# Key and value products from unsplit fp32 operands, and a reordered start, in a two-layer gated attention block

## The chip, the cores and the metric

The kernel runs on one core of a Trainium2 chip. The metric is the device time of one execution in microseconds, the median of several runs. The profile is of one further execution.

## The reference

Two layers over 528 tokens (16 learned ones in front of 512) of width 1024, all in fp32. The parts that matter here:

```python
def hybrid_layer(x, norm_g, w_in, qn_g, kn_g, ...):
    h = rms_norm(x, norm_g)
    proj = jnp.einsum('btd,de->bte', h, w_in)
    q, k, v, gate_a, u_b, gate_b, q_idx, k_idx, w_idx, merge = jnp.split(proj, ...)
    q = apply_rope(rms_norm(q, qn_g), cos, sin)       # 8 heads of 64
    k = apply_rope(rms_norm(k, kn_g), cos, sin)       # one head of 64
    q_idx, k_idx = apply_rope(q_idx, ...), apply_rope(k_idx, ...)
    attn = indexer_sparse_attention(q, k, v, q_idx, k_idx, w_idx, k_top)   # top 128 keys by index score
    y_a = einsum(attn * silu(gate_a), w_a)
    y_b = einsum(multiscale_pool(u_b, ...) * silu(gate_b), w_b)
    g_a, g_b = split(sigmoid(merge))
    return x + einsum(g_a * y_a + g_b * y_b, w_out)
```

The keys `k`, the values `v`, the index key `k_idx` and the index weights `w_idx` are 64 + 64 + 64 + 8 = 200 columns of the input projection.

## The kernel before, in words

**Layout.** The residual `RES` holds the activations transposed: 8 tiles of 128 model dimensions on the partitions, 528 tokens along the free dimension. Tokens are cut in five tiles `TOK` (16, then four of 128) and two halves (the first 272, the last 256).

**Split products.** Most products are made from fp32r operands: an operand is split into a high part (a cast on ScalarE) and a low part (a subtraction), and a product is three matmuls, high by high, low by high, high by low. The normed activations are `nf` (fp32), `hhi` and `hlo`. A weight chunk is fetched as two fp32 halves `raw` (four buffers, so two chunks at a time) and split into tiles `w` (eight buffers, four to a chunk).

**Weights.** `chunks` lists all weight chunks in order of use. `w_load` fetches the next one, on SP's queue. `w_prep_enqueue` puts the splitting of the next one into `prep_q`, whose items run one at each `group_done`; `chunk()` runs what is left and hands the tiles out. When a chunk has been split its `raw` buffers are free and the next `w_load` is issued.

**Order.** The order of instructions on TensorE and VectorE is that of the code. `later(fn, n)` delays a function by n groups. ScalarE, GpSimd and SP are put in order by the scheduler. A row of scales or a transposed tile goes through a PSUM bank (`bank`: three of "d", four of "a", one of "v").

**The start of layer 0.** SP fetches an identity, the 16 tokens, the gains, two x tiles, the key-value chunk, two more x tiles, the rope tables, the head gains and the first index chunk, in that order. `x_half(0)` (L961) squares and sums each x tile on ScalarE, transposes it on TensorE and copies it to `RES`. The key-value chunk is split by ScalarE and GpSimd (L177, L180). `norm_half(0, 0, ...)` (L448) makes `nf` on VectorE (a multiplication by the gain and a row of scales in PSUM), `hhi` on ScalarE, `hlo` on VectorE, two steps behind.

`tok_trio` (L480) then makes keys and values of token tiles 0 to 2 (the first half) side by side: 24 steps of three matmuls of 200 columns. In its middle it calls a hook, which in layer 0 is the work on the other x tiles: `x_half(1)` and the head tables `tables(0)` on GpSimd (L421). Behind it stand `kv_post` (rope, norm and splitting of the keys) and `norm_half(0, 1, ...)`, the norm of the other half. Then come groups of 24 matmuls with `tok_group` (L468): index queries of tiles 1 and 2, keys and values of tiles 3 and 4 (`wk`), index queries of tiles 3 and 4, and the second index chunk, whose splitting is enqueued after the key-value group of tile 4.

**Layer 1** has the same order. Its first norm half is made during layer 0's output projection, where the key-value chunk is split as well; its hooks are the sums of squares and the norm of the second half. Its head tables, `tables(1)`, are issued after layer 0's last gate (L1190), though two of its five instructions run much earlier, where the scheduler found room.

All instructions of TensorE and VectorE are recorded through a helper and have line L60 in the profile; they are told apart by their tiles.

Of the kernel before, what the change touches and what calls it, by code (L numbers as in the profile page):

```python
# [8 lines left out]
F32 = mybir.dt.float32  # L9
# [24 lines left out]
LAG0 = 2  # L34
# [53 lines left out]
def tile_block(ctx: ExitStack, tc: tile.TileContext, x, meta, w_in, pool_w, w_a, w_b, w_out, rows, hgain, c_tab, out):  # L88
# [22 lines left out]
    chunks = []  # L111
    mixed, by_dma = set(), set()
    for l in range(2):
        wi = w_rows(w_in[l], 0, w_in.shape[2])
        chunks.append([(wi[:, :, 512:640], 0), (wi[:, :, 2688:2816], 128)])
        mb = [3784, 4040, 4296, 4552]
        order = [2176, 2432, 1664, 1920, 1408, 1152, 0, 640, 896, 256]
        chunks += [[(wi[:, :, c:c + 256], 0)] for c in order]
        chunks += [[(w_rows(w_b[l], c, 512), 0)] for c in (0, 512)]
        by_dma |= set(range(len(chunks) - 10, len(chunks)))  # L120
        mixed |= set(range(len(chunks), len(chunks) + 8))
        chunks += [[(wi[:, :, c:c + 256], 0)] for c in (*mb, 2760, 3016, 3272, 3528)]
        chunks += [[(w_rows(w_a[l], c, 512), 0)] for c in (0, 512)]
        chunks += [[(w_rows(w_out[l], c, 256), 0)] for c in (0, 256, 512, 768)]
# [3 lines left out]

    def w_load():
        c = W["load"]  # L130
        if c >= len(chunks):
            return
        W["load"] += 1
        kt = chunks[c][0][0].shape[1]
        cols = 2048 // kt
        raws[c] = []
        for s in range(2):
            r = wpool.tile([128, kt // 2, cols], F32, tag="raw", name="raw", bufs=4)
            for src, o in chunks[c]:
                nc.sync.dma_start(r[:, :, o:o + src.shape[2]], src[:, s * kt // 2:(s + 1) * kt // 2, :])  # L140
            raws[c].append(r)

# [11 lines left out]

    def w_prep_enqueue(eng=dve, casts_first=False):
        c = W["prep"]
        if c >= len(chunks):
            return
        W["prep"] += 1
        kt = chunks[c][0][0].shape[1]  # L160
        cols = 2048 // kt
        ready[c] = {}
        if c in mixed:
            prep_q.extend(mixed_prep(c))
            return
        parts = ready[c] = ([], [])

        def split(which):
            t = w_tile().rearrange("p (k e) -> p k e", e=cols)
            parts[which].extend(t[:, k] for k in range(kt // 2))  # L170
            return t

        his = {}

        def high(s):
            his[s] = split(0)
            act.copy(his[s], raws[c][s])  # L177

        def low(s):
            eng.tensor_sub(split(1), raws[c][s], f(his[s]))  # L180
# [12 lines left out]

        def plus(s):
            t = split(0)
            act.copy(t, raws[c][s])
            if s == 1:
                del raws[c]
                w_load()

        def highs():
            high(0)
            high(1)

# [172 lines left out]
    dma(xt[:, 1, :], x[0, 128:256, :])  # L377
    w_load()
    for t in range(2, 4):
        dma(xt[:, t, :], x[0, t * 128:(t + 1) * 128, :])  # L380
    dma(consts[:, 128:], c_tab[:, 128:])
    dma(gains, bass.AP(tensor=hgain.tensor, offset=hgain.offset, ap=[[0, 128], [128, 2], [64, 2], [1, 64]]))
    w_load()
    ident = consts[:, 0:128]
# [35 lines left out]

    def tables(l):  # L421
        gk = tmp.tile([128, 64], F32, tag="gk", name="gk", bufs=1)
        gp.tensor_scalar(gk, gains[:, 1, l], -0.125, None, op0=OP.mult)
        gq = gains[:, 0, l]
# [8 lines left out]
        for tab, g, w in ((Ck, gk, Sk), (Cq, gq, Sq)):  # L433
            gp.tensor_tensor(tab, ctab, bc(g), op=OP.mult)
            gp.tensor_tensor(w.rearrange("p t (a d) -> p t a d", a=2), s4, sw(g), op=OP.mult)

# [30 lines left out]

    def tok_group(t, w, e=256):  # L468
        s, m = TOK[t]
# [9 lines left out]

    def tok_trio(w, mid):  # L480
        hi, lo = H
        pss = [bank("v"), bank("d"), bank("d")]
        first, last_ = range(KT // 2), range(KT // 2, KT)
        for a, b, ks in ((hi, w[0], first), (lo, w[0], first), (hi, w[0], last_), (lo, w[0], last_),
                         (hi, w[1], range(KT))):
            if a is hi and ks is last_:
                mid()
            for k in ks:
                for t in range(3):
                    s, m = TOK[t]  # L490
                    pe.matmul(pss[t][:m, :KV], a[:, k, s:s + m], b[k][:, :KV], start=a is hi and b is w[0] and k == 0,
                              stop=b is w[1] and k == KT - 1)
        return pss

    def dense(w, mt_, a, n, rhs=H, kt=KT, late=False):
# [382 lines left out]
    def mix_gates(zb, ta, s0, n2, operands, splits, alos):  # L878
        base = popped[0] - progress[W["use"]]
        end_ = [None]  # L880
        for q in range(8):
# [23 lines left out]
            def gate(eh, t, src, in_sheet):  # L905
                j = 2 * q + eh
                cs = slice(s0 + t * n2, s0 + (t + 1) * n2)
                if q < 4:
                    th = src if in_sheet else sheet(n2, "th")[:, :n2]
                    act.activation(th, src, AF.Tanh, scale=0.5)  # L910
                    d = zb[:, j, cs]
                    later(lambda: dve.scalar_tensor_tensor(d, th, 1.0, d, op0=OP.add, op1=OP.mult), 2)
                else:
                    end_[0] = act.activation(ta[j - KT][:, cs], src, AF.Tanh, scale=0.5).ins

# [37 lines left out]
            ready.pop(c)  # L953
        return end_[0]

# [5 lines left out]
    def x_half(hf, after=None):  # L961
# [9 lines left out]
        for t in ts_:  # L971
# [3 lines left out]
            for k0 in range(0, KT, kk):  # L975
                tp = bank("v" if t == 0 else "a")
                for k in range(kk):
                    c = (k0 + k) * 128
                    pe.transpose(tp[:, k * m:(k + 1) * m], src[:, c:c + 128], ident[:m, :m])
                (act.copy if (t, k0) == (2, 0) else dve.tensor_copy)(  # L980
                    RES[0][:, k0:k0 + kk, s:s + m], tp[:, :kk * m].rearrange("p (k c) -> p k c", k=kk))
# [5 lines left out]
    x_half(0)  # L987
    w_prep_enqueue(gp)
    flush_prep()
    halved = norm_half(0, 0, rstd, LAG0, ())  # L990

    def second_x():
        x_half(1, halved)
        tables(0)

    hooks = {0: second_x, 1: lambda: norm_half(0, 1, rstd, LAG1)}

    for l in range(2):
        full = [(0, 0, HB, 0), (1, HB, T - HB, 0)]
        halves = full if l == 0 else [(1, 16, T - 16, 0)]  # L1000

        wk = chunk()
        KI[0] = one.tile([128, 2, T], F32R, tag="C", name="KI")
# [7 lines left out]

        pss = tok_trio(wk, hooks[0])
        flush_prep()
        w = chunk(ahead=False)
        for t in range(3):
            later(lambda t=t, ps=pss[t]: kv_post(l, t, ps), 1)
        group_done()
        hooks[1]()
        for what, t in (("q", 1), ("q", 2), ("k", 3), ("k", 4), ("q", 3), ("q", 4)):
            if what == "k":  # L1020
                ps = tok_group(t, wk, KV)
                later(lambda t=t, ps=ps: kv_post(l, t, ps), 1)
            else:
                index_queries(t, 0, w)
            group_done()
            if (what, t) == ("k", 4):
                w_prep_enqueue(casts_first=True)
        w = chunk()
# [154 lines left out]

        gates_end = mix_gates(zb, ta, s0, n2, operands, splits, alos)
# [150 lines left out]
```

## Time and profile before

| | |
|---|---|
| median of 3 runs | 772.63 us (771.91 to 772.87) |
| the profiled execution | 774.25 us |
| its span (first to last instruction) | 772.5 us |
| mean granted TensorE clock | 0.991 |
| TensorE matmul busy | 754.8 us (98%), 5989 instructions |
| VectorE, ScalarE, GpSimd busy | 557.9 (72%), 475.0 (61%), 235.4 (30%) us |
| HBM | 66.41 MB read, 8.55 MB written |

All times in views of the trace are microseconds from the start of the span. In the chain a row is start, length, engine, tile written and line; in the timeline it is start, busy time, engine, line, operation, tile written and tiles read, sizes, count, and in brackets how long the engine stood idle before it and what ended that. A matmul's record includes the way through the array, so records overlap: how long one costs is read from the distance between starts. An fp32 product shows as two records.

### The profile page before, as it was taken

The numbers are of one execution on the slowest core, as the hardware profiler recorded it, in microseconds if no ns is written. First come the engines' busy times: TensorE is split into PE (matmuls) and PEld (weight loads), VectorE is DVE, ScalarE is ACT, GpSimd is POOL, SyncE is SP. The second block draws the span as 40 slices with busy tenths as digits, with TensorE's granted clock in tenths as the row PEclk, the third lists the DMA queues.
The fourth block names the chain that finished last, engine by engine and source line by source line (L and its number), as shares of the span: only waits on it lengthen the run. The fifth ranks groups of instructions, "written<-read, shape, count | busy, mean of one in ns | idle before, by whom it ended". The sixth has DMA issues, their size and how long they took to land.

```text
span 772.5 us, 15843 instructions
## 1 busy us (share of the span) xinstructions
PE 754.8 (98%) x5989; PEld 718.7 (93%) x5989; DVE 557.9 (72%) x1396; ACT 475.0 (61%) x1046; POOL 235.4 (30%) x304
## 2 busy tenths in 40 slices
PE   6999999999999999999999999999999999999998
PEld 5999999999999999999999988988979899999998
DVE  6856787888787786775357658868799887769531
ACT  5577754736788786534244787365668887864420
POOL 6552164425220110043345421652511221104300
PEclk8999999999999999999999999999999999999999
DMA  8538586586022111453513477858721221136311
GB/s 294 183 83 217 140 178 165 125 204 165 2 83 83 55 56 56 149 183 115 161 58 109 111 195 173 192 127 205 183 87 56 75 90 56 56 109 221 129 50 42
DMA packets 73549, 96.96 MB, mean 126 GB/s; under 512 B 3664, under 2 KB 58736, under 8 KB 73472
## 3 DMA queue, kind: packets, MB, share of 16 engines
q1 hardware_dynamic: 67712, 74.97, 30.5%
q0 software_dynamic: 5760, 20.97, 14.8%
q8 instruction: 47, 0.77, 0.4%
q14 instruction: 30, 0.25, 0.1%
HBM read 66.41 MB, written 8.55 MB: 97 GB/s over the span
## 4 chain that ended last, share of the span: by engine, by line
PE 82%; DVE 9%; ACT 5%; POOL 1%; issue 1%; DMA 1%; SPq 0%; DVEq 0%; ACTq 0%; POOLq 0%
PE d L60 67%; PE a L60 11%; PE v L60 4%; DVE w L60 2%; DVE nf L60 1%; ACT lt L691 1%; DVE hlo L60 1%; ACT w L222 1%; DVE t L60 1%; DVE sc L60 1%; DMA hsheet<-far 1%; DVE alo L60 0%; DMA xt<-in_x_dram 0%; DVE raw L60 0%; DVE m L60 0%
## 5 line engine op out<-in xcount | busy, mean ns | idle before, releaser
L60 PE MATMUL d<-hhi,w 128*128 128x256 f32 (+3 forms) x1408 | 289.8, 297 | 0.0
L60 PEld LDWEIGHTS d<-hhi,w 128*128 128x128 f32 x1408 | 226.3, 188 | 7.0 <-issue 1.6
L60 PE MATMUL d<-hlo,w 128*128 128x256 f32 (+3 forms) x704 | 193.6, 294 | 0.6 <-POOL hlo L1202 0.6
L60 PE MATMUL d<-w,hhi 128*128 128x256 f32 (+2 forms) x928 | 145.8, 286 | 2.0 <-DVE w L60 0.9
L60 PEld LDWEIGHTS d<-hlo,w 128*128 128x128 f32 x704 | 132.5, 188 | 3.3 <-POOL hlo L1202 0.8
L60 PEld LDWEIGHTS d<-w,hhi 128*128 128x128 f32 (+1 forms) x928 | 125.8, 187 | 6.4 <-ACT hhi L462 2.2
L60 DVE TENSOR_TENSOR w<-raw,w 128x512 fp32r<-128x512 f32 (+1 forms) x130 | 110.0, 857 | 2.2 <-ACT w L222 2.1
L703 POOL TENSOR_SCALAR pm<-lt,rs 128x16 f32<-128x16 f32 x64 | 40.3, 644 | 183.1 <-DVE rs L60 169.2
L60 PE MATMUL d<-w,hlo 128*128 128x256 f32 (+2 forms) x464 | 85.2, 282 | 0.0
L60 PE MATMUL d<-hsum,w 128*128 128x264 f32 (+1 forms) x576 | 77.8, 286 | 0.0
L60 PEld LDWEIGHTS d<-hsum,w 128*128 128x128 f32 x576 | 72.0, 188 | 1.5 <-issue 0.7
L60 PEld LDWEIGHTS d<-w,hlo 128*128 128x128 f32 (+1 forms) x464 | 68.0, 187 | 0.4
L192 POOL DMA_DIRECT2D w<-raw x40 | 36.4, 925 | 104.0 <-ACT w L191 83.4
L222 ACT CAST w<-raw 128x512 fp32r<-128x512 f32 x96 | 56.3, 623 | 2.9 <-DVE raw L60 2.9
L1202 POOL TENSOR_TENSOR hlo<-ta,hhi 128x256 fp32r<-128x256 f32 (+1 forms) x32 | 31.1, 988 | 82.0 <-ACT hhi L1201 82.0
L60 DVE MATCH_REPLACE8 sc<-m,sc 128x400 f32<-128x400 f32 (+2 forms) x100 | 54.3, 548 | 0.0
L60 DVE MAX8 m<-sc 128x8 f32<-128x400 f32 (+2 forms) x100 | 52.7, 556 | 0.8
L691 ACT ACTIVATE lt<-lt,mn,NR 128x144 f32<-128x144 f32 (+3 forms) x64 | 42.4, 665 | 12.0 <-DVE mn L60 12.0
L60 PE MATMUL d<-mhi,w 128*128 128x272 f32 (+2 forms) x192 | 48.9, 331 | 0.4 <-ACT zb L1163 0.4
L191 ACT ACTIVATE w<-raw 128x1024 fp32r<-128x1024 f32 x40 | 41.3, 1057 | 11.3 <-PE d L60 11.3
L60 DVE SCALAR_TENSOR_TENSOR sc<-r,wsg,sc 128x144 f32<-128x144 f32 (+3 forms) x56 | 32.4, 581 | 15.5 <-ACT r L615 13.2
L580 POOL TENSOR_TENSOR t<-t,t 128x256 f32<-128x256 f32 (+1 forms) x34 | 30.8, 907 | 39.2 <-DVE t L60 39.2
(199 smaller groups left out, 1372.4 us busy)
## 6 DMA issues: line engine op xcount, KB each, us to landing
raw<-in_w_in_dram SPq DMA_DIRECT2D x72, 512.0 KB, 3.9
w<-raw POOLq DMA_DIRECT2D x40, 512.0 KB, 5.9
raw<-in_w_out_dram SPq DMA_DIRECT2D x16, 512.0 KB, 3.4
kept<-res SPq DMA_DIRECT2D x16, 264.0 KB, 2.5
res<-kept SPq DMA_DIRECT2D x16, 264.0 KB, 6.5
raw<-in_w_branch_b_dram SPq DMA_DIRECT2D x8, 512.0 KB, 4.4
raw<-in_w_branch_a_dram SPq DMA_DIRECT2D x8, 512.0 KB, 3.5
xt<-in_x_dram SPq DMA_DIRECT2D x4, 512.0 KB, 5.3
```

The lines of the kernel that those rows point to most:

```text
L60: return fn(*a, **k)
L191: act.activation(t, raws[c][s], AF.Copy, scale=-1.0)
L192: gp.dma_start(t, raws[c][s], accum_op=OP.add)
L222: act.copy(t[:, 0], blk[src[n]])
L580: gp.tensor_tensor(t1[:m, :256], t1[:m, :256], t2[:m, :256], op=OP.add)
L691: act.activation(L[hh][:, :n], L[hh][:, :n], AF.Exp, scale=NR[:, i, h:h + 1], bias=mn[:, hh:hh + 1], accum_out=sm[:, hh:hh + 1])
L703: gp.tensor_scalar(pms[i][:, 2 * j + hh, :], L[hh][:, 0:16], rs[:, hh:hh + 1], None, op0=OP.mult)
L1202: gp.tensor_sub(hlo[:, j, a:a + n], d, f(hhi[:, j, a:a + n]))
```

## The change

The key-value chunk of each layer is no longer split. It is second in the order of chunks, behind the first index chunk; its products are made by TensorE from `nf` and `raw` directly, as one fp32 matmul for each token tile and model tile instead of three fp32r ones. Its `raw` buffers are held until the key-value group of tile 4.

At the start, SP fetches the first half of the key-value chunk, the tables and head gains, its second half, the first index chunk, and only then the last two x tiles. The first norm makes all eight `nf` before its eight `hlo`. The first index chunk is split behind them (casts on ScalarE, subtractions on VectorE; GpSimd splits nothing). `x_half(1)` stands behind the products of tiles 0 to 2 instead of in their middle, with two of its four copies on ScalarE, and the norm of the second half behind the first index-query group. Two more dummy matmuls (`spin(2)`) stand in front of the first x tile's transposes. The casts of the second index chunk in layer 0 are issued after the second norm's last cast, and `tables` is called for keys and queries apart; `tables(1)` is issued after the last `hlo` of layer 0's gate stage.

```diff
+        chunks.append([(wi[:, :, 2176:2432], 0)])
+        plain.add(len(chunks))
         chunks.append([(wi[:, :, 512:640], 0), (wi[:, :, 2688:2816], 128)])
-        order = [2176, 2432, 1664, 1920, 1408, 1152, 0, 640, 896, 256]
+        order = [2432, 1664, 1920, 1408, 1152, 0, 640, 896, 256]
...
+        if c in plain:
+            return
...
         def highs():
-            high(0)
-            high(1)
+            with tc.issue_after(after) if after else nullcontext():
+                high(0)
+                high(1)
...
     dma(xt[:, 1, :], x[0, 128:256, :])
-    w_load()
+    first, kv = w_place(), w_place()
+    w_fetch(kv, 0)
+    dma(consts[:, 128:], c_tab[:, 128:])
+    dma(gains, ...)
+    w_fetch(kv, 1)
+    for s in range(2):
+        w_fetch(first, s)
     for t in range(2, 4):
         dma(xt[:, t, :], x[0, t * 128:(t + 1) * 128, :])
-    dma(consts[:, 128:], c_tab[:, 128:])
-    dma(gains, ...)
-    w_load()
...
-    def tok_trio(w, mid):
...
+    def plain_mm(ps, t, k, raw):
+        s, m = TOK[t]
+        pe.matmul(ps[:m, :KV], NF[0][k // 4][:, k % 4, s:s + m], raw[k // 4][:, k % 4, :KV], start=k == 0,
+                  stop=k == KT - 1)
+
+    def plain_trio(raw, mid):
         pss = [bank("v"), bank("d"), bank("d")]
+        for k in range(KT):
+            if k == 3:
                 mid()
+            for t in range(3):
+                plain_mm(pss[t], t, k, raw)
         return pss
+
+    def plain_group(t, raw):
+        ps = bank("d")
+        for k in range(KT):
+            plain_mm(ps, t, k, raw)
+            if k == 3:
+                half_done()
+        return ps
...
                 tp = bank("v" if t == 0 else "a")
+                if (t, k0) == (1, 0):
+                    spin(2)
...
-                (act.copy if (t, k0) == (2, 0) else dve.tensor_copy)(
+                (act.copy if (t, k0) in ((2, 0), (3, 4), (4, 4)) else dve.tensor_copy)(
...
     x_half(0)
-    w_prep_enqueue(gp)
-    flush_prep()
-    halved = norm_half(0, 0, rstd, LAG0, ())
-
-    def second_x():
-        x_half(1, halved)
-        tables(0)
-
-    hooks = {0: second_x, 1: lambda: norm_half(0, 1, rstd, LAG1)}
+    halved = norm_half(0, 0, rstd, KT, ())
+    tables(0, True)
+    hooks = {0: lambda: None}
...
-        pss = tok_trio(wk, hooks[0])
-        flush_prep()
-        w = chunk(ahead=False)
+        kv = W["use"] + 1
+        pss = plain_trio(raws[kv], hooks[0])
+        if l == 0:
+            w_prep_enqueue(True)
+        w = chunk()
+        W["use"] += 1
+        if l == 0:
+            x_half(1, halved)
         for t in range(3):
             later(lambda t=t, ps=pss[t]: kv_post(l, t, ps), 1)
         group_done()
-        hooks[1]()
+        if l:
+            hooks[1]()
         for what, t in (("q", 1), ("q", 2), ("k", 3), ("k", 4), ("q", 3), ("q", 4)):
             if what == "k":
-                ps = tok_group(t, wk, KV)
+                ps = plain_group(t, raws[kv])
                 later(lambda t=t, ps=ps: kv_post(l, t, ps), 1)
             else:
                 index_queries(t, 0, w)
+                if (l, t) == (0, 1):
+                    halved = norm_half(0, 1, rstd, LAG1)
             group_done()
             if (what, t) == ("k", 4):
-                w_prep_enqueue(casts_first=True)
+                del raws[kv]
+                w_load()
+                w_prep_enqueue(True, None if l else halved)
+                if l == 0:
+                    tables(0, False)
...
-        if l == 0:
-            with tc.issue_after(gates_end):
-                tables(1)
...
-                    gp.tensor_sub(hlo[:, j, a:a + n], d, f(hhi[:, j, a:a + n]))
+                    split_end = gp.tensor_sub(hlo[:, j, a:a + n], d, f(hhi[:, j, a:a + n]))
...
         if l == 0:
+            with tc.issue_after(split_end.ins):
+                tables(1, True)
+                tables(1, False)
```

More of the change, by code (lines that the diff above doesn't have):

```diff
@@ L111, in tile_block @@
     chunks = []
-    mixed, by_dma = set(), set()
+    mixed, by_dma, plain = set(), set(), set()
     for l in range(2):
         wi = w_rows(w_in[l], 0, w_in.shape[2])
+        chunks.append([(wi[:, :, 2176:2432], 0)])
+        plain.add(len(chunks))
         chunks.append([(wi[:, :, 512:640], 0), (wi[:, :, 2688:2816], 128)])
         mb = [3784, 4040, 4296, 4552]
-        order = [2176, 2432, 1664, 1920, 1408, 1152, 0, 640, 896, 256]
+        order = [2432, 1664, 1920, 1408, 1152, 0, 640, 896, 256]
         chunks += [[(wi[:, :, c:c + 256], 0)] for c in order]
@@ L127, in tile_block, with w_place, w_fetch, w_load @@
     raws, ready = {}, {}
-    def w_load():
+    def w_place():
         c = W["load"]
-        if c >= len(chunks):
-            return
         W["load"] += 1
         kt = chunks[c][0][0].shape[1]
[L135 to L141, printed above, removed]
+        raws[c] = [wpool.tile([128, kt // 2, 2048 // kt], F32, tag="raw", name="raw", bufs=4) for s in range(2)]
+        return c
+    def w_fetch(c, s):
+        kt = chunks[c][0][0].shape[1]
+        for src, o in chunks[c]:
+            nc.sync.dma_start(raws[c][s][:, :, o:o + src.shape[2]], src[:, s * kt // 2:(s + 1) * kt // 2, :])
+    def w_load():
+        if W["load"] < len(chunks):
+            c = w_place()
+            for s in range(2):
+                w_fetch(c, s)
     prep_q = deque()
@@ L153, in w_tile, with w_prep_enqueue @@
         return wpool.tile([128, 1024], F32R, tag="w", name="w", bufs=8)
-    def w_prep_enqueue(eng=dve, casts_first=False):
+    def w_prep_enqueue(casts_first=False, after=None):
         c = W["prep"]
@@ L179, in low @@
         def low(s):
-            eng.tensor_sub(split(1), raws[c][s], f(his[s]))
+            dve.tensor_sub(split(1), raws[c][s], f(his[s]))
             if s == 1:
@@ L377, in tile_block @@
     dma(xt[:, 1, :], x[0, 128:256, :])
-    w_load()
+    first, kv = w_place(), w_place()
+    w_fetch(kv, 0)
+    dma(consts[:, 128:], c_tab[:, 128:])
+    dma(gains, bass.AP(tensor=hgain.tensor, offset=hgain.offset, ap=[[0, 128], [128, 2], [64, 2], [1, 64]]))
+    w_fetch(kv, 1)
+    for s in range(2):
+        w_fetch(first, s)
     for t in range(2, 4):
         dma(xt[:, t, :], x[0, t * 128:(t + 1) * 128, :])
-    dma(consts[:, 128:], c_tab[:, 128:])
-    dma(gains, bass.AP(tensor=hgain.tensor, offset=hgain.offset, ap=[[0, 128], [128, 2], [64, 2], [1, 64]]))
-    w_load()
     ident = consts[:, 0:128]
@@ L419, in sheet, with tables @@
         return tmp.tile([128, HB], F32, tag="tt", name=name, bufs=6)
[L421 to L424, printed above, removed]
+    def tables(l, keys):
+        if keys:
+            gk = tmp.tile([128, 64], F32, tag="gk", name="gk", bufs=1)
+            gp.tensor_scalar(gk, gains[:, 1, l], -0.125, None, op0=OP.mult)
+        tab, g, w = (Ck, gk, Sk) if keys else (Cq, gains[:, 0, l], Sq)
         def bc(g):
@@ L432, in tables @@
         s4 = stab.rearrange("p t (a d) -> p t a d", a=2)
-        for tab, g, w in ((Ck, gk, Sk), (Cq, gq, Sq)):
-            gp.tensor_tensor(tab, ctab, bc(g), op=OP.mult)
-            gp.tensor_tensor(w.rearrange("p t (a d) -> p t a d", a=2), s4, sw(g), op=OP.mult)
+        gp.tensor_tensor(tab, ctab, bc(g), op=OP.mult)
+        gp.tensor_tensor(w.rearrange("p t (a d) -> p t a d", a=2), s4, sw(g), op=OP.mult)
     def inv_rms(o, i, eng=gp):
@@ L466, in norm_half, with tok_group @@
         return end.ins
-    def tok_group(t, w, e=256):
+    def tok_group(t, w):
+        e = 256
         s, m = TOK[t]
@@ L478, in tok_group @@
         return ps
-    def tok_trio(w, mid):
-        hi, lo = H
+    def plain_mm(ps, t, k, raw):
[3 more added lines that the diff above has]
+    def plain_trio(raw, mid):
         pss = [bank("v"), bank("d"), bank("d")]
[L483 to L486, printed above, removed]
+        for k in range(KT):
+            if k == 3:
                 mid()
[L488 to L492, printed above, removed]
-        return pss
+            for t in range(3):
+                plain_mm(pss[t], t, k, raw)
+        return pss
+    def plain_group(t, raw):
[5 more added lines that the diff above has]
+        return ps
     def dense(w, mt_, a, n, rhs=H, kt=KT, late=False):
@@ L879, in mix_gates @@
         base = popped[0] - progress[W["use"]]
-        end_ = [None]
         for q in range(8):
@@ L913, in gate @@
                 else:
-                    end_[0] = act.activation(ta[j - KT][:, cs], src, AF.Tanh, scale=0.5).ins
+                    act.activation(ta[j - KT][:, cs], src, AF.Tanh, scale=0.5)
             def total(eh, t, ps, part):
@@ L953, in mix_gates @@
             ready.pop(c)
-        return end_[0]
     ss0 = one.tile([128, 5], F32, name="ss0")
@@ L1000, in tile_block @@
         halves = full if l == 0 else [(1, 16, T - 16, 0)]
-        wk = chunk()
         KI[0] = one.tile([128, 2, T], F32R, tag="C", name="KI")
@@ L1182, in alos @@
                 dve.tensor_sub(alo[:, :, a:a + n], sa[:, :, a:a + n], f(ahi[:, :, a:a + n]))
-        gates_end = mix_gates(zb, ta, s0, n2, operands, splits, alos)
+        mix_gates(zb, ta, s0, n2, operands, splits, alos)
         drain()
```

## The prediction

> **What bounds the kernel now.** I read the page's engine table, then the chain that ended last, the stretches by granted clock, and the waits. The page first:
>
> ```profile
> PE 754.8 (98%) x5989; PEld 718.7 (93%) x5989; DVE 557.9 (72%) x1396; ACT 475.0 (61%) x1046; POOL 235.4 (30%) x304
> ...
> GB/s 294 183 83 217 140 178 165 125 204 165 2 83 83 55 56 56 149 183 115 161 58 109 111 195 173 192 127 205 183 87 56 75 90 56 56 109 221 129 50 42
> ```
>
> TensorE is busy for 98% of the span of 772.5 us. An edit far from a PE gap is therefore worth only its TensorE time, and an edit at a gap is worth at most that gap. The chain of the first 60 us (start, length, what) shows where the gaps are:
>
> ```profile
> 9.93 1.31 DVE nf L60 x3
> 11.24 1.71 DVE hlo L60
> ...
> 18.09 3.41 PE a L60 x16
> ...
> 26.48 0.09 PE v L60
> 26.57 0.22 PE d L60 x2
> ```
>
> From 9.93 to 18.09 the chain runs through VectorE, which makes `nf` and the low halves `hlo`. TensorE gets its 72 key-and-value products (24 steps of three, 0.31 us a step in the last two rows) only as these arrive. Undisturbed, 24 steps are 7.5 us. They lie between 10.9 and 26.9, with 3.4 us of transposes inside. The stretches by clock (length, PE, PEld, DVE, ACT, POOL busy, granted clock, DMA share, GB/s) show a second loss:
>
> ```profile
> 12.35:15.77 3.42, 2.39 (x11) 1.88 (x12) 3.42 (x4) 0.62 (x2) 3.08 (x3) 0.50 1.04 335
> 15.77:19.18 3.41, 3.16 (x16) 2.67 (x16) 3.41 (x8) 1.71 (x5) 3.41 (x5) 0.50 1.10 356
> 19.18:22.59 3.41, 3.41 (x18) 3.30 (x17) 3.41 (x7) 3.38 (x6) 2.34 (x4) 0.50 0.30 96
> ...
> 326.40:329.80 3.40, 1.55 (x13) 1.33 (x12) 2.83 (x6) 0.82 (x2) 0.00 (x0) 1.00 0.88 263
> 329.80:333.20 3.40, 3.40 (x18) 3.40 (x17) 1.30 (x3) 0.42 (x1) 0.76 (x1) 0.50 1.03 368
> ```
>
> The granted clock is 0.50 for three stretches, from 12.35 to 22.59, while TensorE waits and then while it recovers. This start is what the change works on. TensorE from the first index-query group on:
>
> ```profile
> 27.09 1.20 PE L60 MATMUL d<-w,hhi 128*128 128x256 f32 x8
> ...
> 38.22 1.11 PE L60 MATMUL d<-w,hhi 128*128 128x200 f32 x8
> ...
> 40.06 2.02 PE L60 MATMUL d<-w,hhi 128*128 128x200 f32 x16
> ...
> 47.02 0.46 PE L60 MATMUL a<-identr,qs 128*128 128x128 f32 x4
> ...
> 52.24 0.75 PE L60 MATMUL d<-w,hhi 128*128 128x256 f32 x4 [0.93 <-DVE w L60]
> ```
>
> The key group of token tile 4 runs from 38.22. Sixteen of its matmuls take it to 40.06, so all 24 end at 40.98 (2.76 us). Two query groups then end at 47.02 (2.9 us each, with a few transposes). One more gap, 0.93, waits for VectorE's split of the second index weights.
>
> **The change, part by part.** First the price of an unsplit fp32 product, which the kernel has already, though with 272 and 256 or 128 columns instead of 200:
>
> ```profile
> 114.70 1.05 PE L60 MATMUL a<-us,pw 128*128 128x272 f32 x4
> 115.40 0.47 PE L60 MATMUL d<-hhi,w 128*128 128x272 f32 x1
> 115.71 0.28 PE L60 MATMUL d<-hlo,w 128*128 128x272 f32 x1
> ```
>
> ```profile
> 211.28 1.16 PE L60 MATMUL v<-ptm,BV 128*128 128x128 f32 x8
> 212.19 0.37 PE L60 MATMUL d<-hhi,w 128*128 128x264 f32 x1
> ```
>
> The trace shows two records for each fp32 product (four records for two `us,pw` products of 272 and 256 columns). From 114.70 to 115.71 are 1.01 us; less one split product (about 0.12) that is 0.22 a record of 264 columns, so 0.168 for 200. The eight `ptm,BV` records of 128 columns take 0.114 each (211.28 to 212.19). The bounds for 200 columns are thus 0.114 and 0.22. I take 0.168, since time grows with the columns from one row to the other. A product is 0.336 against three split ones (0.31): a step of three is 1.01 against 0.94, the first pass over tiles 0 to 2 8.1 against 7.5, and a key group 2.69 against 2.76. TensorE alone therefore loses 0.6 per layer.
>
> The start of layer 0 gains. The products now need `nf` alone, no cast and no low half, and raw weights, no split. GpSimd's weight subtraction, beside which a single `hlo` took the 1.71 quoted, is gone. VectorE makes its eight `nf` in a row at 0.44 (1.31 for three), from the same 9.93 on, ending at 13.4. TensorE starts at 10.4 and spends 1.01 a step, slower than the supply. At full clock it ends at 18.5. The transposes of the last two x tiles follow at 18.5 and take 1.7 instead of 3.41 at the half clock: 20.2. Three things must be there in time.
>
> The first is the data. Both x tiles now stand behind the first index weights and the tables on SP: 4.9 MB lie ahead of their end. The page's first slice (19.3 us) moves 5.7 MB, and 0.8 MB less at 356 GB/s is 17.1. That is 1.4 us of cover; without it each us of lateness counts in full.
>
> The second is the split of the first index weights, which VectorE now has behind eight `hlo`:
>
> ```profile
> 18.62 2.11 DVE L60 TENSOR_TENSOR hlo<-nf,hhi 128x272 fp32r<-128x272 f32 x3
> 20.65 2.47 DVE L60 COPY res<-a 128x512 f32<-128x512 f32 x4
> 23.05 1.21 DVE L60 TENSOR_TENSOR w<-raw,w 128x1024 fp32r<-128x1024 f32 x1
> ```
>
> Eight `hlo` at 0.4 (the chain's undisturbed ones) to 0.7 (here, beside GpSimd's tables), two splits at 1.2 and two copies at 0.62 end between 20.7 and 23. The first query group takes hhi, then hlo, and needs the low weights only after 16 products (22.1). The two copies moved to ScalarE queue there behind the square of the last x tile, which comes behind the first key square: they end near 21.5, ahead of the next norm.
>
> The third is VectorE after the first query group (20.2 + 2.9 = 23.1), where the second norm's row of scales is now transposed on TensorE:
>
> ```profile
> 27.33 0.21 DVE L60 TENSOR_TENSOR t<-v,Ck 16x64 f32<-16x64 f32 x1 [1.94 <-ACT sq L516]
> ...
> 30.03 1.25 DVE L60 SCALAR_TENSOR_TENSOR nf<-res,parT,a 128x256 f32<-128x256 f32 x3
> ...
> 36.39 1.08 DVE L60 TENSOR_TENSOR ks<-t,ks 16x256 fp32r<-16x256 f32 x3
> ```
>
> From the first `nf` of the second half to the last key split are 7.4 us (30.03 to 37.47), and TensorE went on to the key group of tile 4 at 38.22, 0.75 later. Now `nf` can start at 23.4, so this group starts at 31.6. TensorE's own work (a query group 2.9, a key group 2.7, small transposes 1.3) would bring it there by 30.2: a new gap of 1.4 us, with the whole PE queue behind it. The group ends at 34.3 instead of 40.98: **6.7 us gained**.
>
> The gap of 0.93 should go too. Ahead of that VectorE split, the chain of before runs over GpSimd:
>
> ```profile
> 45.09 1.10 POOL Ck L434
> 46.19 0.83 POOL Sk L435
> ```
>
> These are layer 1's tables; the change issues them after the last low half of layer 0's gate stage. Without them VectorE comes 1.9 us earlier, more than 0.93: **0.9 gained**. In their new place GpSimd adds squares while TensorE has a whole output projection in front of it; I price that at nothing. If that cover were gone the cost would be their own length, some 4 us. The spin before the x tiles fills a wait for DMA: nothing.
>
> In layer 1 TensorE stood still before this stage for almost nothing, so the 0.6 counts: **0.6 lost**. The weight splits no longer made there free VectorE and ScalarE, which TensorE did not wait for.
>
> Sum: -6.7 - 0.9 + 0.6 = -7.0. The profiled execution (span 772.5, time 774.25) would be 767.25. Its time lies 1.6 above the median of 772.63, where the same 7.0 gives **765.6**.
>
> **The rivals.** *The half clock stays for a while.* Until the first `nf` is there at 10.4 TensorE still stands idle for about 1 us, about a third of a stretch of 3.41. The stretch at 326.40, with 1.55 busy of 3.40, was followed by one at 0.50; the one at 15.77, with 3.16 busy by records, did not lift it. A third idle lies between these. Each stretch at half clock costs 3.41/2 = 1.7, and one and a half cost 2.6: 767.3 to 768.2. The timed runs may also have had one such stretch less than the profile (1.6 less time), with the same result for the median. The Trainium skill, "TensorE: Matmul & The Clock Gate", section "Why this matters for your kernels", asks only for no idle gaps over about 3 us; by that the clock would hold and the sum stay as it is. The trace disagrees: its stall at 327 was 1.85 us, and half clock followed.
>
> *The first norm is slow for another reason.* If `hlo` beside the tables takes the 1.71 of the chain instead of 0.7 for three of the eight, or the x tiles come 2 us late, VectorE or DMA replaces the old wait: up to 3 us, 768.6.
>
> *Slower: the weight load of the fp32 product is not hidden.* There are 80 such records per layer, 160 in all. If each paid a load of 0.114 on top of its stream, that is 18 us: 783. It decides from 7.0/160 = 0.044 us a record. Against it: 128-column records follow each other in 0.114, load and stream together. The Trainium skill, same page, section "Weight-path perf modes", says that fast weight load is not given to fp32, which speaks for this rival; the 0.114 of the trace does not.
>
> *Nothing comes of it.* If the second half of the raw weights or `nf` paces the products as the low halves did, the time stays near 772.
>
> **How the numbers follow.** Forecast 0.52, half clock 0.26, slow norm 0.12, nothing 0.04, slower 0.06. A measurement of this kernel tells about 0.2% (1.5 us) from no change. The low end of the range is the forecast without the new gap (1.4) and with layer 1 at no loss (0.6), rounded down by 0.6 for splits that no longer load VectorE: 763.0. The high end is the two clock cases and the slow norm, 768.8. Left out are the last two cases and some of the rest. Faster 0.90, same 0.04, slower 0.06.
>
> **What would show it.** Right: in the profile after, `raw,nf` matmuls from about 10.4 on with no wait on `hhi` or `hlo`, records 0.168 apart, the x transposes near 18.5, the key group of tile 4 starting near 31.6 behind a gap on `ks`, no gap on `w` near 44, and PEclk near full through the first slices. Wrong: records over 0.21 apart, an xt wait in front of the transposes, a granted clock of 0.50 past 16 us, or a later stage than the first index queries that lost time.

## The result and the profile after

The changed kernel takes 770.53 us (median of 20 runs, 769.57 to 772.92), the kernel before, in as many runs beside it, 773.24 us (771.91 to 776.21). The ratio is 0.9961, with an interval of 0.9951 to 0.9971: 0.4% faster, where 0.9% was forecast. The profiled execution after took 769.85 us, with a span of 768.1. From the page after, TensorE's row and the granted clock in tenths:

```profile
PE 753.9 (98%) x5911; PEld 710.9 (93%) x5911; DVE 552.7 (72%) x1392; ACT 472.1 (61%) x1044; POOL 228.7 (30%) x302
...
PEclk9999999999999999999999999999999999999999
```

TensorE is as busy as before (98%), over a span 4.4 us shorter. The first key-value pass and what follows, in the timeline of TensorE after (start, busy time, operation; in brackets the idle time before it):

```profile
10.85 0.51 PE L60 MATMUL v<-raw,nf 128*16 128x200 f32 x2 [0.67 <-DVE nf L60]
11.29 0.94 PE L60 MATMUL d<-raw,nf 128*128 128x200 f32 x4
12.17 0.51 PE L60 MATMUL v<-raw,nf 128*16 128x200 f32 x2
12.61 0.94 PE L60 MATMUL d<-raw,nf 128*128 128x200 f32 x4
13.48 0.51 PE L60 MATMUL v<-raw,nf 128*16 128x200 f32 x2
...
21.29 1.91 PE L60 MATMUL a<-consts,xt 128*128 128x128 f32 x16
22.95 1.20 PE L60 MATMUL d<-w,hhi 128*128 128x256 f32 x8
...
28.94 2.87 PE L60 MATMUL d<-raw,nf 128*128 128x200 f32 x16
31.74 0.43 PE L60 MATMUL a<-VM,consts 16*128 16x64 f32 x2
33.05 1.19 PE L60 MATMUL a<-identr,ks 16*128 16x16 f32 x11 [0.56 <-DVE ks L60]
34.08 2.94 PE L60 MATMUL d<-raw,nf 128*128 128x200 f32 x16
36.72 1.25 PE L60 MATMUL d<-w,hhi 128*128 128x256 f32 x8
...
42.91 0.46 PE L60 MATMUL a<-identr,qs 128*128 128x128 f32 x4
...
47.32 0.46 PE L60 MATMUL a<-identr,ks 128*128 128x128 f32 x4
```

The order of events is the one forecast, with no wait on `hhi` or `hlo`, the transposes in 1.66 us (21.29 to 22.95) and a small gap on `ks`. But a step of the pass, from one `v` row to the next, takes 1.32 us (12.17 to 13.48) where 1.01 was forecast, and the whole pass 10.44 (10.85 to 21.29) where 8.1 was. The key groups of tiles 3 and 4 are also unsplit fp32 products, of the same 200 columns, and they run as forecast (2.69): 16 records in 2.80 (28.94 to the next row at 31.74), and 2.64 from 34.08 to the next group at 36.72.

So the dear products are those of tile 0, which has 16 tokens (`128*16`), beside those of 128 tokens. The number of tokens, which is the number of rows a product writes, is called its width below. Within a step the starts of the six records are 0.18, 0.26, 0.27, 0.17, 0.17 and 0.26 us apart: three of six come 0.1 us late, two at the passage from 16 to 128 tokens and one at the passage back.

Layer 1 before, then after (TensorE's timeline: the key-value pass, and the key group of tile 3 up to the small transposes behind it):

```profile
402.56 0.25 PE L60 MATMUL v<-w,hhi 128*16 128x200 f32 x1
...
411.05 0.38 PE L60 MATMUL a<-consts,msq 128*128 128x128 f32 x2
...
418.63 0.75 PE L60 MATMUL d<-w,hhi 128*128 128x200 f32 x2 [0.37 <-ACT hhi L462]
...
421.11 0.43 PE L60 MATMUL a<-VM,consts 16*128 16x64 f32 x2
```

```profile
396.68 0.51 PE L60 MATMUL v<-raw,nf 128*16 128x200 f32 x2
...
407.90 0.38 PE L60 MATMUL a<-consts,msq 128*128 128x128 f32 x2
...
416.60 0.43 PE L60 MATMUL a<-VM,consts 16*128 16x64 f32 x2
```

The pass grew from 8.49 (402.56 to 411.05) to 11.22 (396.68 to 407.90). From its end to the end of the key group of tile 3 it fell from 10.06 to 8.70: before, this group waited for the casts of the second half's norm (its fourth to seventh records start 0.25 to 0.73 us apart, against 0.11 undisturbed; the rows mark 0.37 of it as idle), and now it needs none.

One more row of before closes the interval that held the gap of 0.93:

```profile
52.83 0.46 PE L60 MATMUL a<-identr,ks 128*128 128x128 f32 x4
```

The ledger, from the same matmuls in both profiles:

| place | forecast | found |
|---|---|---|
| start to the end of the last index-query group (47.02 before, 42.91 after) | -6.7 | -4.11 |
| from there to the second `identr,ks` row (5.81 us before, from 47.02 to 52.83; 4.41 after, from 42.91 to 47.32) | -0.9 | -1.40 |
| a gap near 186 that grew from 0.38 to 1.34 | 0 | +0.96 |
| the stretch at half clock near 330, in the profile before only | 0 | -1.53 |
| layer 1, key-value pass | +0.6 | +2.73 |
| layer 1, up to the end of the key group of tile 3 | 0 | -1.36 |
| sum; end of the span | -7.0 | -4.71; -4.4 |

Shifts of under 0.35 us make up the rest. Without the clock stretch the span is some 2.9 us shorter, close to what the medians say (2.7).

The gap near 186, in ScalarE's timeline after, in TensorE's, and in the chain of work that ended there (SP's issue of a weight fetch, then the transfer behind it):

```profile
186.71 0.63 ACT L868 CAST hhi<-hsheet 128x528 fp32r<-128x528 f32 x1 [4.00 <-DMA hsheet<-far]
187.24 0.65 ACT L1189 COPY zb<-d 128x272 f32<-128x272 f32 x2
```

```profile
187.67 0.38 PE L60 MATMUL d<-mhi,w 128*128 128x256 f32 x1 [1.34 <-ACT zb L1189]
```

```profile
182.42 0.08 SPq L142
...
182.55 4.13 DMA hsheet<-far
```

ScalarE stood 4.0 us at one copy, whose data SP fetched only behind a fetch of raw weights (L142). SP itself waited 4.5 and 1.8 us ahead of its last two weight fetches here, and the profile puts both waits down to the transfer `w<-raw`, which reads the raw buffers. Behind that copy waited the `zb` copies that empty TensorE's banks. Before, the same copy waited as well, 2.37 us, but TensorE came there later and lost 0.38.

### The profile page after: what moved, and what is told of

It is laid out like the page before. It is cut to its first block, busy times and chain, and to the rows that moved or that the text cites. A ratio compares the mean times of both kernels' runs of the same rounds, so it can differ in the third digit from the quotient of the medians.

```text
span 768.1 us, 15671 instructions
## 1 busy us (share of the span) xinstructions
PE 753.9 (98%) x5911; PEld 710.9 (93%) x5911; DVE 552.7 (72%) x1392; ACT 472.1 (61%) x1044; POOL 228.7 (30%) x302
## 4 chain that ended last, share of the span: by engine, by line
PE 85%; DVE 9%; ACT 4%; issue 1%; POOL 1%; DMA 1%; DVEq 0%; POOLq 0%; ACTq 0%; SPq 0%
PE d L60 69%; PE a L60 11%; PE v L60 5%; DVE w L60 2%; DVE nf L60 1%; ACT w L232 1%; DVE t L60 1%; DVE sc L60 1%; ACT lt L712 1%; DVE m L60 1%; DMA hsheet<-far 1%; DVE ta L60 1%; DVE alo L60 0%; DVE hlo L60 0%; DVE raw L60 0%
## 5 line engine op out<-in xcount | busy, mean ns | idle before, releaser
L60 PE MATMUL d<-w,hhi 128*128 128x256 f32 (+1 forms) x800 | 124.7, 286 | 0.0
L60 PEld LDWEIGHTS d<-w,hhi 128*128 128x128 f32 (+1 forms) x800 | 107.4, 185 | 2.8 <-issue 1.2
L60 DVE TENSOR_TENSOR w<-raw,w 128x512 fp32r<-128x512 f32 (+1 forms) x128 | 107.7, 851 | 2.2 <-ACT w L232 2.1
L60 PE MATMUL d<-w,hlo 128*128 128x256 f32 (+1 forms) x400 | 74.5, 281 | 0.0
L60 PEld LDWEIGHTS d<-w,hlo 128*128 128x128 f32 (+1 forms) x400 | 58.4, 184 | 0.4
```

The lines of the kernel that those rows point to most:

```text
L60: return fn(*a, **k)
```

## The experiments

The theory from these rows: a change of width between fp32 products costs TensorE about 0.1 us, so the tile of 16 tokens is what makes the pass dear. Rivals: fp32 records in turn over three banks are dear whatever their width, or the pass waits for data. The first four kernels start from the changed kernel.

**wide128**: tile 0 computed over 128 tokens, of which only 16 are used.

```diff
 def plain_mm(ps, t, k, raw):
-    s, m = TOK[t]
+    s, m = TOK[t] if t else (0, 128)
```

> The product of token tile 0 is made over 128 tokens instead of 16; the rows beyond 16 are not used. Same number of products, same three PSUM banks in turn, same streams of 200 columns. In the changed kernel a step of three takes 1.32 us, with gaps of 0.26 to 0.27 at each passage between the 16-wide product and the 128-wide ones and 0.168 elsewhere. Theory A (the array is emptied when an fp32 product of 16 columns follows one of 128 or the other way round): the step falls to 1.01, the pass over tiles 0 to 2 from 10.5 to 8.1 us in both layers, and the time by 4 to 5 us to about 766. Theory B (going from bank to bank costs): steps stay 1.32, the time stays at 770.5. Theory C (the 16-wide product itself is slow, the 128-wide ones are not hurt by it): the two 128-wide products keep their 0.87 and the step is 1.21, the time falls by 1.7 us.

766.18 us (765.22 to 767.65, 6 runs), ratio to before 0.9905, interval 0.9888 to 0.9921. Its pass in the timeline:

```profile
12.18 0.50 PE L60 MATMUL v<-raw,nf 128*128 128x200 f32 x2
12.52 0.84 PE L60 MATMUL d<-raw,nf 128*128 128x200 f32 x4
13.20 0.50 PE L60 MATMUL v<-raw,nf 128*128 128x200 f32 x2
...
19.29 0.93 PE L60 MATMUL a<-consts,xt 128*128 128x128 f32 x7
```

A step is 1.02 us, all records are 0.169 apart, and the pass, from 11.06 on, takes 8.23. With eight times the tokens in tile 0 the pass is 2.2 us shorter. In layer 1 it takes 9.01 (394.54 to 403.55) against 11.22:

```profile
394.54 0.50 PE L60 MATMUL v<-raw,nf 128*128 128x200 f32 x2
...
403.55 0.38 PE L60 MATMUL a<-consts,msq 128*128 128x128 f32 x2
```

The span is 4.4 shorter than after.

**run16**: the eight products of tile 0 in one run, ahead of those of tiles 1 and 2, so that the width changes once.

```diff
         for k in range(KT):
-            if k == 3:
-                mid()
-            for t in range(3):
+            plain_mm(pss[0], 0, k, raw)
+        mid()
+        for k in range(KT):
+            for t in (1, 2):
                 plain_mm(pss[t], t, k, raw)
```

> The eight products of token tile 0 come first, in a run; then tiles 1 and 2 in turn. Theory A: one passage per layer instead of sixteen, so all records 0.168 apart but for one or two; layer 0 waits a little for nf at the start (0.44 against 0.34 a step), so the time is 0.3 to 0.8 above the kernel with 128-wide products, 766 to 767. Theory B: tiles 1 and 2 still change bank with each product, so two thirds of the loss stay, about 769. Theory C: the slow product is as slow in a run, the time stays near 770.5.

767.46 us (766.59 to 768.31, 6 runs), ratio 0.9917, interval 0.9901 to 0.9933. The products keep their 16 tokens:

```profile
13.32 1.51 PE L60 MATMUL v<-raw,nf 128*16 128x200 f32 x8 [1.09 <-DVE nf L60]
14.77 5.68 PE L60 MATMUL d<-raw,nf 128*128 128x200 f32 x32
20.29 1.91 PE L60 MATMUL a<-consts,xt 128*128 128x128 f32 x16
```

32 records from 14.77 to 20.29 are 0.17 each, and the eight of 16 tokens are no cheaper. So neither the narrow product nor the turn over banks is dear; the alternation is. This order outruns VectorE's `nf`, hence the wait of 1.09, which is of the size of its distance to wide128 (1.28 in the medians, whose intervals overlap).

**wide64** and **wide96**: as wide128, with 64 and 96 tokens.

> Token tile 0's product over 64 tokens. Theory A with the loss tied to a product that takes half of the array or less: step 1.32 as with 16. If only very narrow products (32 or less) cost, step 1.01.

> Token tile 0's product over 96 tokens. Theory A with the loss tied to a narrow part of the array (up to half of it): no loss, step 1.01, as with 128. If any change of width costs, the step stays at 1.32.

One run each: 771.72 and 766.43 us. The timelines of wide64 and of wide96:

```profile
12.24 0.94 PE L60 MATMUL d<-raw,nf 128*128 128x200 f32 x4
13.12 0.55 PE L60 MATMUL v<-raw,nf 128*64 128x200 f32 x2
13.60 0.94 PE L60 MATMUL d<-raw,nf 128*128 128x200 f32 x4
```

```profile
13.94 0.84 PE L60 MATMUL d<-raw,nf 128*128 128x200 f32 x4
14.61 0.50 PE L60 MATMUL v<-raw,nf 128*96 128x200 f32 x2
14.95 0.84 PE L60 MATMUL d<-raw,nf 128*128 128x200 f32 x4
```

With 64 tokens a step is 1.36 (12.24 to 13.60), with 96 it is 1.01: the loss depends on the width, and its bound lies between 64 and 96. The Trainium skill, "TensorEngine Tiling (Array Packing)", section "Key Properties", says that a change of tiling mode drains TensorE; in the list of modes of the same page (section "Available Configurations") the widest below the full 128 columns has 64. The two fp32 rows fit that rule, if a narrow product counts as such a mode; the fp32r products of 16 tokens in the kernel before, which alternate with wide ones at 0.31 us a step, show no such loss. That it is this drain which costs the 0.1 us is therefore not shown. The prediction did not weigh such a rule.

**The order without the unsplit products, and the other way round.** unsplit_old is the kernel before with the unsplit products alone (128 tokens for tile 0), in the old order: chunks, x tiles, hooks and tables as before.

```diff
+        plain.add(len(chunks))
...
-        pss = tok_trio(wk, hooks[0])
+        pss = plain_trio(raws[kv], hooks[0])
...
-                ps = tok_group(t, wk, KV)
+                ps = plain_group(t, raws[kv])
```

> The kernel before with one thing changed: keys and values as unsplit fp32 products from nf and raw, token tile 0 over 128 tokens. Order of fetches, first norm (nf and hlo alternating), transposes in the middle of the products, tables and copies stay as before. Theory F (the unsplit product alone brings the start's gain): nf comes every 0.85 us against 1.01 a step, the products with the transposes in their middle end near 21, the second index weights still wait 0.9: time about 767 to 768. Theory G (the order is needed): the products wait for nf or the transposes for a bank, the half clock comes back, time 770 or more.

771.2 us (769.39 to 776.97, 12 runs), ratio 0.9977, interval 0.996 to 0.9995. The timeline of TensorE there:

```profile
33.86 1.19 PE L60 MATMUL a<-identr,ks 16*128 16x16 f32 x11 [1.09 <-DVE ks L60]
34.88 4.62 PE L60 MATMUL d<-raw,nf 128*128 128x200 f32 x16
```

The second key group starts at 34.88, 3.3 us ahead of before (38.22) and 2.8 behind wide128 (32.07); in this execution it also fell into a stretch at half clock (16 records in 4.62). By the medians the unsplit products bring 0.2% and the new order the other 0.7% of wide128's gain; which part of the new order brings it was not tried. From the last index-query group (45.39) to the second `identr,ks` row (49.79) are 4.40 us here, as in the changed kernel: the unsplit products alone, with all tables where they were before, already take the gap of 0.93 away.

**w128_nospin**: wide128 without `spin(2)`.

```diff
-                if (t, k0) == (1, 0):
-                    spin(2)
```

> The kernel with 128-wide products without the two dummy matmuls in front of the x transposes. If they keep the clock up: granted clock of 0.50 for one stretch or more behind 12 us, 1.7 us a stretch, time 767.5 to 769. If the products' own pace holds the clock: 1.00 from about 9 to 10 us on as with them, and the transposes begin 0.15 earlier, time 766.0.

767.77 us (765.8 to 769.25, 6 runs), ratio 0.9923, interval 0.9905 to 0.9941. Its first steps:

```profile
11.92 1.54 PE L60 MATMUL d<-raw,nf 128*128 128x200 f32 x4
13.26 0.87 PE L60 MATMUL v<-raw,nf 128*128 128x200 f32 x2
```

Four records take 1.34 us, 0.33 each: half clock, up to 14.6. The unchanged wide128 did the same in its second profile (w128_again, below), so what the two spins do for the clock is not settled.

**w128_tabold** and **w128_qtab**: wide128 with all of `tables(1)`, or its query part alone, issued after the last gate again.

```diff
+        if l == 0:
+            with tc.issue_after(gates_end):
+                tables(1, True)       # w128_tabold only
+                tables(1, False)
...
             with tc.issue_after(split_end.ins):
-                tables(1, True)       # w128_tabold only
-                tables(1, False)
```

> The same, with all of layer 1's tables issued after the last gate, as before the change. The prediction's step: with Ck and Sk back on GpSimd between the key groups and the second index weights, VectorE's split of these is late again and a gap of about 0.9 returns in front of a d<-w,hhi product some 15 us behind the key groups; the time is 0.9 to 1.4 above the kernel with only the query tables back. Rival: the split is in time now that VectorE is less behind; no gap, no difference.

> The kernel with 128-wide products, and the two query tables of layer 1 (Cq, Sq) issued after the last gate again, as before the change; its key tables (gk, Ck, Sk) stay behind the last low half. All kernels with the changed order show a gap of 1.3 to 1.4 us near 186 in front of a product from mhi, against 0.38 before; there GpSimd made these two tables before the change. Theory D (the gap comes from the tables' move): back to about 0.4, time 1.0 lower than with 128-wide products alone, about 765.2. Theory E (it comes from the stage running 5 us earlier against its transfers): the gap stays, time 766.2.

w128_tabold: 766.38 us (765.6 to 767.23, 5 runs), ratio 0.9905, interval 0.989 to 0.992. w128_qtab: 767.66 us (767.03 to 768.1, 5 runs), ratio 0.9921, interval 0.9907 to 0.9936. From w128_tabold, GpSimd's and TensorE's timelines:

```profile
36.23 0.88 POOL L447 TENSOR_TENSOR Ck<-consts,gk 128x320 f32<-128x320 f32 x1
```

```profile
40.34 0.46 PE L60 MATMUL a<-identr,qs 128*128 128x128 f32 x4
...
44.75 0.46 PE L60 MATMUL a<-identr,ks 128*128 128x128 f32 x4
...
185.34 0.39 PE L60 MATMUL d<-mhi,w 128*128 128x256 f32 x1 [1.19 <-ACT zb L1191]
```

The key tables (`Ck` here) are back in this stage, though some 2 us further ahead of the end of the last query group, and the interval is 4.41 us (40.34 to 44.75) as in the changed kernel: as in unsplit_old, the gap of 0.93 goes without taking them away. The gap near 186 is there whether the tables are late or early (1.19 here, 1.37 in w128_qtab), so they do not make it.

**w128_late**, **w128_again** and **before_again**, on one chip: wide128 with the second copy one entry later in its list; wide128 itself; and one more profile of the kernel before.

```diff
         late = deque([lambda: fetch(1, 0), lambda: fetch(1, 1), lambda: high(1, 0), lambda: low(1, 0),
-                      lambda: high(1, 1), lambda: low(1, 1), lambda: fetch(0, 0), lambda: fetch(0, 1)])
+                      lambda: fetch(0, 0), lambda: high(1, 1), lambda: low(1, 1), lambda: fetch(0, 1)])
```

> wide128 with one entry of the list `late` of sums_of_h moved: the second `hhi<-hsheet` copy comes one output tile later, behind the third fetch. Theory E (the gap of about 1.3 near 186 is ScalarE standing at that copy, in front of the `zb` copy that frees a bank): the gap falls under 0.4 and the time is about 1 us below wide128 on the same chip, near 765. Rival (E'): the bank is late for another reason, or the same wait comes back one item later or at `hsum`: the sum of the gaps between 170 and 215 stays within 0.3 of wide128's and so does the time.

> wide128 unchanged, timed on the same chip as w128_late: about 766, span 763 to 765, the gap in front of `d<-mhi,w` near 185.6 at 1.2 to 1.4, layer 0's first pass from 11 to 19 with records 0.169 apart.

> The kernel before, profiled once more and unchanged. If the half clock of its start (12.35 to 22.59) and the stretch at 0.50 near 330 belong to the kernel, both are there again; if they are chance, one or both are gone and the span is 1.5 to 3 us shorter. The gap in front of `d<-mhi,w` near 186 should be 0.3 to 0.5 again if it depends on when the stage runs.

w128_late: 767.56 us (766.99 to 768.16, 4 runs), ratio 0.9921, interval 0.9908 to 0.9935. w128_again: 768.1 us (765.43 to 769.17, 5 runs), ratio 0.9917, interval 0.9901 to 0.9933. One and the same kernel thus has medians of 766.18 and 768.1, so differences of 1 to 2 us between these variants are not settled by their medians; they are read from the traces. The copy in w128_late:

```profile
184.42 0.63 ACT L868 CAST hhi<-hsheet 128x528 fp32r<-128x528 f32 x1 [4.36 <-DMA hsheet<-far]
```

It waits as long as ever, and the gap is 1.70 (a stretch at half clock follows it, from 185.6 to 189.0). The scheduler, which orders ScalarE and SP, left both as they were, so this run tells nothing about the theory.

before_again took 773.01 us, span 771.2. The stretches by granted clock around 330, with the same columns as in the prediction:

```profile
326.40:329.80 3.40, 1.55 (x12) 1.33 (x11) 2.75 (x6) 0.81 (x2) 0.00 (x0) 1.00 0.83 249
329.80:333.20 3.40, 3.40 (x30) 3.40 (x29) 2.21 (x5) 0.83 (x2) 0.94 (x2) 1.00 1.05 380
```

The same 1.55 us of work, the same 1.85 of idling, and no half clock behind it. So the -1.53 of the ledger belongs to the execution, not to the change. The gap near 186 is 0.19 here, less than the 0.3 expected, with a wait of 1.73 at the copy. The start of this execution, in its timeline:

```profile
17.20 0.63 PE L60 MATMUL d<-w,hlo 128*128 128x200 f32 x2
...
22.03 0.39 PE L60 MATMUL d<-w,hhi 128*128 128x200 f32 x2
```

Two records take 0.63 until 21, 0.39 later, and the transposes between them start 0.213 us apart up to 21.0 and 0.110 behind it: half clock up to about 21, although the stretches by granted clock show 1.00 there. The spacing of the records decides. The start in half clock is thus in both profiles of before.

**w128_actq**: wide128 with the fetch for that copy, in layer 0, issued by ScalarE instead of SP.

```diff
-                dma(t, far[:, w, g, k.start - 2 * g:k.stop - 2 * g])
+                (nc.scalar.dma_start if (l, w, g) == (0, 1, 1) else dma)(
+                    t, far[:, w, g, k.start - 2 * g:k.stop - 2 * g])
```

> wide128 with one DMA on another queue: in layer 0 the fetch of the second `hsheet` for `hhi` is issued by ScalarE, some 3.5 us before SyncE came to it, instead of by SyncE behind a fetch of raw weights; its copy on ScalarE stands one place further ahead. Theory E (the gap near 185 is ScalarE waiting at that copy for its data, because SyncE stood behind the raw fetch): the copy no longer waits past 182.5 and the gap in front of `d<-mhi,w` near 185 falls from 1.3 to under 0.4; that is 1 us, about 0.13% of the time. Rival (E'): the bank is late for another reason, or the wait goes to another copy: gaps between 170 and 215 add up to within 0.3 of those of wide128 and its second profile (1.3 and 1.6).

764.31 us (763.91 to 767.26, 6 runs), ratio 0.9889, interval 0.9871 to 0.9907: the lowest median of all versions, though the interval overlaps that of wide128. The spans of the two profiles are 762.3 and 763.7. ScalarE, then TensorE:

```profile
180.54 0.63 ACT L868 CAST hhi<-hsheet 128x528 fp32r<-128x528 f32 x1 [1.37 <-DMA hsheet<-far]
```

```profile
183.54 0.56 PE L60 MATMUL a<-KK,qq 128*128 128x144 f32 x4
183.94 0.33 PE L60 MATMUL d<-mhi,w 128*128 128x256 f32 x1
```

The copy is done at 181.2 and TensorE goes on without a gap. The scheduler also put the copy one operation further ahead in ScalarE's order; that operation was done at 180.7 in wide128, 4 us before the data came there, so it is the earlier fetch that counts. The gap near 186 was SP's queue: a fetch standing behind a weight fetch whose buffer is not free. The changed kernel comes there some 5.5 us earlier than before and loses more. The other kernels fit that roughly: unsplit_old comes 2.6 us earlier and loses 0.87, the two profiles of wide128 come 7.5 and 5.8 us earlier and lose 1.31 and 1.58, so the loss does not grow steadily. What sets the time of the weight fetch was not tried.

## Why the prediction was wrong

- **Bound and direction** held: the start was the place, TensorE no longer waits for `hhi` or `hlo` there, and the kernel is faster.
- **The price of the first pass** is the step that failed: "I take 0.168", a record, "the first pass over tiles 0 to 2 8.1". In the pass a record measured 0.22 (1.32 a step of six), and the pass took 10.44 us. The key groups, priced by the same row, came out (16 records in 2.64 to the next group, forecast 2.69). The prediction had both ends, 0.114 and 0.22, and the pass met the upper one by coincidence: 0.22 was the price of a record of 264 columns, while records of 200 cost 0.169 here wherever the width does not alternate. The range did not take the upper end in, since 0.05 more on 48 records in two layers is 5 us. The rows it was priced from were all of products of 128 tokens. In the split kernel the 16-token products alternated with wide ones at no visible cost (a step of three in 0.31), so nothing quoted showed the price; the prediction took that for fp32 too.
- **The start** gave 4.11 instead of 6.7. TensorE began the pass at 10.85 instead of 10.4 (VectorE's first `nf` came at 10.30, not 9.93) and lost 2.3 in it; with that, every later time is 2.4 to 2.8 late (transposes 21.29 for 18.5, key group of tile 4 34.08 for 31.6, its end 36.72 for 34.3). The index split ended at 19.59, ahead of the forecast 20.7 to 23, and from the first `nf` of the second norm to the key group of tile 4 were 7.8 us (26.29 to 34.08), forecast 8.2. The data were in time, but not as priced: the two x tiles landed at 17.46 and 18.71, not by 17.1, so the "1.4 us of cover" at 18.5 was not there. It cost nothing, here or in wide128, where they landed by 18.56 and the transposes began at 19.29. The gap on `ks` was 0.56, forecast 1.4. Two sums are slightly off, with no effect: the terms named for VectorE add up to 20.2 to 22.6, and 765.6 and 18 are 783.6, not 783.
- **The gap of 0.93** went, which was luck as far as its reason goes: the reason given, that the tables leave GpSimd there, is not what it needs. w128_tabold and unsplit_old have the tables in that stage and no gap.
- **Layer 1** "+0.6" was +2.73 in the pass, and -1.36 that the prediction missed: it said TensorE waited "for almost nothing" there, and the key group of tile 3 waited for casts. With 128 tokens the pass costs +0.52 (9.01 against 8.49), as priced.
- **"The rest at nothing"** missed the gap near 186, +0.96.
- **The rivals.** Half clock at the start did not show in the profile after. It does in one of the two profiles of wide128: one had full clock from the first record of the pass on, the other from 14.5, and its last index-query group starts its transposes 1.76 us later (0.18 of that from a later start of the pass). The fp32 weight load was hidden, as the key groups show. A slow norm and "nothing comes of it" did not happen.

## What to carry to other kernels

Price an instruction from a row of its own shape and of its own neighbours: here the same record cost 0.169 us in a run and 0.22 on the mean where the width alternated, and computing 112 tokens that nobody needs saved 4.4 us. When a stage comes earlier, look for the transfer that is issued behind another one on its queue: it does not come earlier with it.

## What the runs showed of the hardware

- fp32 products of 16 or 64 output rows in turn with ones of 128 lose about 0.1 us at a change of width (steps of 1.32 and 1.36 instead of 1.01 us); with 96 none. The fp32r products of 16 and 128 in the kernel before show no such loss (0.31 us for a step of three).
- The granted clock is not a property of the kernel alone. The same gap of 1.85 us near 325 is in all fourteen profiles; in eight of them a stretch of 3.4 us at half clock followed, in six none did. The kernel before and wide128, profiled twice each, are once on either side. The two profiles of wide128 have spans of 763.7 and 767.4 us: 1.76 us of the difference is there by the end of the index queries, 1.45 comes from that stretch.
- A fetch on SP's queue came no earlier than the weight fetch in front of it, which waited for its buffer; on ScalarE's queue it was issued at 174.97 instead of 180.37, and a gap of 1.31 us on TensorE went.
